# Block products of a seven-product multiply: where their results lie in PSUM, and a planning margin for the side work's TensorE steps

## The chip, the cores and the metric

The kernel runs on one core of one Trainium2 chip. The metric is the device time of one execution in microseconds (us); less is better. Several executions are timed, and their median is the kernel's time. One more execution is recorded by the hardware profiler, and all rows of the profile come from that one.

## The reference

The program is one inference step of a two-layer recurrent decoder trunk for 512 prompt tokens and 8 sample tokens, which the kernel treats as 520 columns. The change lies in layer 1 (HGRN2). Cut to what matters:

```python
def layer_c(h, p, s_c, lb, norm_w, w_in, c_norm_w, w_out, ple_w, ple_g):
    u = rmsnorm(h, norm_w) @ w_in
    q, fx, v, gate = jnp.split(u, [HK_C, 2 * HK_C, 2 * HK_C + D_C], axis=-1)
    g = jnp.logaddexp(jnp.log(lb), jnp.log1p(-lb) + jax.nn.log_sigmoid(fx))
    k = (1.0 - lb) * jax.nn.sigmoid(-fx)
    ...
    o, new_c = hgrn2_scan(q * (DK_C ** -0.5), k, v, g, s_c)
    o = o * lax.rsqrt(jnp.mean(o * o, axis=-1, keepdims=True) + EPS)
    o = o.reshape(Bsz, L, D_C) * c_norm_w * jax.nn.silu(gate)
    h = h + o.astype(h.dtype) @ w_out
    ...
```

There are 16 heads of 128 channels each, so `w_in` is a 1024 x 8192 matrix in four parts q, f, v and g (gate) of 2048 columns. The numbers are 32-bit floats.

## The kernel before

**Layout and precision.** Activations lie with channels on the 128 partitions and the 520 tokens along the free axis. To multiply 32-bit floats, each operand is split into a high and a low part of the type that TensorE takes at its faster rate (`fp32r`), and three products are summed: high x high, high x low, low x high. The split of a weight tile is an ACT cast (`whi` or, from layer 1 on, `whir`) and a DVE subtraction (`wlo`, `wlor`). These go through a small ring of buffers (`ring_space`, line 640; `split_half`, line 645).

**Layer 1** (`layer1_fast`, line 1611) works on pairs of heads, `pr` = 0 to 7. For each pair it makes the projections f, v, q and g; then `decay` computes the decays of the pair, `head` does the chunked recurrence of one head, and `samples` does the 8 sample tokens of the pair. After pairs 2, 4 and 6, inside `pair`, `chunk` multiplies finished heads with the output matrix; the rest follows at the end (`o7`, `o8`).

**The seven-product multiply.** For pairs 1 to 7, f and v are not computed as plain products. `strassen` (line 1705) takes the weights of the two heads, 1024 x 256, as 2 x 2 blocks of 512 x 128, and the activations, 1024 x 520, as 2 x 2 blocks of 512 x 260. Seven block products then do what eight would do in the plain way; the price is additions of blocks before (in DVE, on the weights: `s2`, `s3` and two in place) and after (the results p1 to p7 are copied or added into the pair's tiles `l1a` for f and `l1b` for v). One block product (`product`) is 4 steps over k, each with three matmuls of 128 x 128 by 128 x 260 that add up in PSUM. One call of `strassen` makes f and v of a pair, so 14 block products, n = 0 to 13, in the order p1, p6, p7, p2, p5, p3, p4, first for f, then for v. There are seven calls, 98 block products and 1176 matmuls in all. In the profile their result is the tile `sm`.

**PSUM.** There are two kinds of places. `mmps` gives a tile of two halves of 512 words each (`[128, 2, 512]`), and two such tiles take turns (tag `mm`). All main products use them: a plain product has its 520 columns in the two halves, 260 each. `grab` gives one of four single places of 512 words (`ax0` to `ax3`, called banks in the planner) for the side work: the tiles `A`, `kt`, `kv`, `o`, `ot` and `vt` of the heads, `vs` and `os` of the samples. Before the change, `strassen` opens a new two-half tile for every second product: products 0 and 1 lie in the halves of one tile, 2 and 3 in the next, and so on.

**What sets the order.** The kernel records all operations and a planner (`Plan`, line 210) then lays out the instruction queues. It simulates all engines with a table of costs (`COST`) and takes at each moment the ready operation with the smallest due time `prio`. Main products (`block(True)`) advance a position `pos` by their length; side work is given an offset to that position (`side(start, rate)`), and `urgency` draws it forward where a main product depends on it. Dependencies in the plan go by overlapping regions (`_meet`), so the two halves of a tile are independent there. A new `mm` tile waits for all users of the tile two before it. For a single place, `hold_banks` also asks that all that its readers need from earlier has been queued before its first use; a product that finds no place free is passed over for the moment (`pick`). The resulting order of each engine is fixed in the program; on the chip each engine goes through its queue in order and waits on semaphores that the framework under the kernel sets by its own dependency tracking.

**The margin.** `later(spare)` marks the operations recorded under it. When such an operation runs on TensorE and depends on one of another engine, the planner takes it to be ready `spare` us later than it would be. Nothing is added to the program; only the order changes. Before the change it is used in layer 0 only (0.5, 4.0 and 1.0).

The heads' five TensorE steps, in order, are `A` (scores), `kt` (transposes), `kv`, `o` and `ot` (transposes), and between them lie steps of DVE, ACT and POOL. The TensorE steps of `samples` are `vs`, `os` and a small `ot..s`.

Of the kernel before, what the change touches and what calls it, by code (L numbers as in the profile page):

```python
# [26 lines left out]
HN = N // 2  # L27
# [182 lines left out]
class Plan:  # L210
# [31 lines left out]
    @contextmanager  # L242
    def side(self, start=0.0, rate=0.0, pinned=False):

        keep = self.shift, self.rate, self.pinned
        self.shift, self.rate, self.pinned = start, rate, pinned
        yield
        self.shift, self.rate, self.pinned = keep
# [15 lines left out]
    @contextmanager  # L264
    def block(self, main=False):

        self.open = Op(self, self.pos + self.shift, 0)
        self.open.forms["pe"] = [[], 0.0, None]
        self.open.main = main
        self.open.ins, self.open.outs = [], []  # L270
        yield
        op, self.open = self.open, None
        op.forms["pe"][1] /= 2400.0
        self.add(op, op.ins, op.outs)
# [261 lines left out]
V_LATE, DECAY_LATE, SAMPLE_LATE, HEAD_LATE = 6.67, 0.0, 2.75, -9.44  # L536
HEAD_I, HEAD_RATE, N1_LATE = 6.15, 0.14, -61.78
# [3 lines left out]
def hybrid_decode_step_kernel(ctx: ExitStack, tc: tile.TileContext, I, O, mode="both"):  # L541
# [18 lines left out]
    plans = [Plan(engines, pools, [f"ax{i}" for i in range(4)])]  # L560
    act, dve, pool, pe, sp = (Engine(plans, k) for k in ("act", "dve", "pool", "pe", "sp"))
    side, block = (lambda *a, **k: plans[-1].side(*a, **k)), (lambda *a: plans[-1].block(*a))

    def new(pool_, shape, tag, name, bufs=1, dt=F32):
        return plans[-1].tile(pool_, shape, dt, tag, name, bufs, {"psm": PSUM, "psa": PSUM, "drp": DRAM}.get(pool_, SBUF))
# [4 lines left out]
    def mmps(name):  # L570
        return new("psm", [128, 2, 512], "mm", name, 2)

    def grab(name):

        return new("psa", [128, 512], "ax", name)
# [10 lines left out]
    def tt(out, a, b, op, eng=dve):  # L586
        eng.tensor_tensor(out=out, in0=a, in1=b, op=op)
# [13 lines left out]
    def copy(out, in_):  # L601

        plans[-1].record(("act", "copy", (out, in_), {}), ("dve", "tensor_copy", (out, in_), {}))
# [25 lines left out]
    def load_group(g):  # L629
        ap, k0, kk, c, w = groups[g]  # L630
        r = new("wp", [128, 2048], "raw", f"wraw{g}", 2)
        v = r[:, :kk * w].rearrange("p (k c) -> p k c", k=kk)
        with side(*((plans[-1].shift, 0.0, True) if plans[-1].pinned else (-LOAD_AHEAD,))):
            sp.dma_start(out=v, in_=ap[k0 * 128:(k0 + kk) * 128, c:c + w].rearrange("(k p) c -> p k c", p=128))
        raw_of[g] = v
# [9 lines left out]
    def split_half(v):  # L645

        hv, lv = (r.rearrange("p (k c) -> p k c", k=4) for r in ring_space(1))
        with side(-SPLIT_AHEAD):
            act.copy(hv, v)
            tt(lv, v, hv.bitcast(F32), SUB)  # L650
        return hv, lv
# [300 lines left out]
    mx, e0, e1, sm, lb, omlb, lb60, oml60, lbf, omf, cneg, cq, ch, fb = (lbt[:, i] for i in range(14))  # L952
# [658 lines left out]
    def layer1_fast():  # L1611
# [92 lines left out]

        def strassen(pr, names):

            ps, n = None, 0

            def product(u, x):
                nonlocal ps, n  # L1710
                if n % 2 == 0:
                    ps = mmps(f"sm{pr}_{n // 2}")
                out = ps[:, n % 2, :HN]
                n += 1
                hw, lw = u
                for k in range(4):
                    with block(True):
                        for i, (w, b) in enumerate(((hw, x[0]), (hw, x[1]), (lw, x[0]))):
                            pe.matmul(out, lhsT=w[:, k], rhs=b[:, k], start=(k == 0 and i == 0), stop=(k == 3 and i == 2))
                    plans[-1].pos += 0.334  # L1720
                return out

            def steps(nm):
                e, e1 = 2 * pr, 2 * pr + 1
                start, done = (start_f, done_f) if nm == "f" else (start_v, done_v)
                o0, o1 = start(e), start(e1)
                l0, r0, l1, r1 = o0[:, :HN], o0[:, HN:], o1[:, :HN], o1[:, HN:]
                g = units[sec[f"{nm}{pr}"]][0]
                if g not in raw_of:
                    load_group(g)  # L1730
                v = raw_of[g]
                a11, a12, a21, a22 = v[:, :4, :128], v[:, 4:, :128], v[:, :4, 128:], v[:, 4:, 128:]
                s2, s3 = (new("cst", [128, N], "sgt", f"{nm}{pr}s{i}", 2)[:, :512].rearrange("p (k c) -> p k c", k=4)
                          for i in range(2))
                w = split_half(a11)
                with side(-SPLIT_AHEAD):
                    tt(s3, a11, a21, ADD)
                    tt(a21, a21, a22, ADD)
                    tt(s2, a21, a11, ADD)
                p1 = product(w, x11)  # L1740
                copy(l0, p1)
                p6 = product(split_half(s2), u2)
                tt(r0, l0, p6, ADD)
                p7 = product(split_half(s3), t3)
                tt(l1, p7, r0, SUB)
                w = split_half(a12)
                with side(-SPLIT_AHEAD):
                    tt(a12, a12, s2, ADD)
                p2 = product(w, x21)
                tt(l0, l0, p2, ADD)  # L1750
                p5 = product(split_half(a21), u1)
                tt(r1, l1, p5, SUB)
                tt(r0, r0, p5, ADD)
                p3 = product(split_half(a12), x22)
                tt(r0, r0, p3, ADD)
                done(e)
                p4 = product(split_half(a22), u4)
                tt(l1, l1, p4, ADD)
                done(e1)

            for nm in names:
                steps(nm)
# [147 lines left out]
        def pair(pr, names):  # L1910
            a = 2 * pr
            if pr:
                strassen(pr, names[:2])
                with side(DECAY_LATE):
                    decay(a)
                names = names[2:]
            for nm in names:
                ev = {"f": evac_f, "v": evac_v, "q": evac_q, "g": evac_g}[nm]
                tiles = [(sec[f"{nm}{pr}"] + i, 0, ev(a + i), f"{nm}{a + i}") for i in range(2)]
                if pr == 0 and nm == "f":  # L1920
                    project_both(tiles, XN, K8)
                else:
                    for t in tiles:
                        project_both([t], XN, K8)
                if nm == "f":
                    with side(DECAY_LATE):
                        decay(a)
                if nm == "q" and pr in (2, 4, 6):
                    chunk(f"o{pr}", 2 * pr - 4, 2 if pr == 6 else 4, add_to_h)

        for pr in range(8):
            pair(pr, "fvqg")
            with side(SAMPLE_LATE):
                samples(2 * pr)
            for i in range(2):
                with side(HEAD_LATE + i * HEAD_I, HEAD_RATE):
                    head(2 * pr + i)
        last, o_ = None, last
        chunk("o7", 10, 4, add_to_h)
# [184 lines left out]
    def layer1_end(pl1, ytk, ytk4, keep, pre):  # L2124
# [49 lines left out]
        for half, (sl, blocks) in enumerate(HALVES):  # L2174
# [16 lines left out]
            for i in blocks[:2]:  # L2191
# [5 lines left out]
        act.dma_start(out=O["y_s"].rearrange("b o d -> (b o) d"), in_=ytk4[120:])  # L2197

    layer1_fast()
    layer1_end(slot("xa", "pl1"), slot("w", "ytk", [128, 4160])[:, :4 * D].rearrange("p (i d) -> p i d", i=4),  # L2200
               new("cst", [128, D], "misc", "ytk4"),
# [53 lines left out]
```

## Time and profile before

| | |
|---|---|
| median of 3 runs | 1092.01 us (1089.67 to 1096.3) |
| the profiled execution's own time | 1095.35 us |
| its span, first to last instruction | 1093.6 us |
| TensorE busy (matmul), share of the span | 95% |
| TensorE busy (weight loads) | 92% |
| VectorE (DVE) busy | 78% |
| ScalarE (ACT) busy | 54% |
| GpSimd (POOL) busy | 13% |
| mean granted TensorE clock | 0.992 |
| from and to HBM | 125 GB/s over the span |

PE is the matmul row of TensorE and PEld its weight-load row, which overlaps it. The page also shows the span in 40 equal slices of 27.3 us; each digit is the busy share in tenths:

```profile
PE   8999899999999999999998998989999999999995
PEld 8889898899999999999888998989989889899995
DVE  6788788998977556897797877788867789878863
ACT  6588775645563122555474635455455546564553
```

Layer 0 takes the slices up to about the 17th. Pairs 1 to 7 of layer 1 lie between the 19th and the 38th. PE drops to 8 in several slices of layer 1. The groups of the block products, by what they read, among the costliest groups of the page (busy us, mean ns of one, then idle time of the engine just before them and what ended most of it):

```profile
L520 PE MATMUL sm<-uh,whir 128*128 128x260 f32 x224 | 65.6, 293 | 8.3 <-DVE l1b L520 5.7
L520 PE MATMUL sm<-xh,whir 128*128 128x260 f32 x168 | 50.9, 303 | 14.0 <-DVE l1a L520 14.0
L520 PE MATMUL sm<-ul,whir 128*128 128x260 f32 x224 | 63.4, 283 | 0.0
L520 PE MATMUL sm<-uh,wlor 128*128 128x260 f32 x224 | 63.2, 282 | 0.0
```

All operations are recorded by one helper, so every row has its line (L520), and groups are told apart by their tiles. `xh`, `xl` and `uh`, `ul` are high and low parts of the activation blocks and of their combinations; `whir` and `wlor` are high and low parts of the weights. The first of the three matmuls of a k-step reads `uh` or `xh` with `whir`; the idle time stands before these alone.

### The profile page before, as it was taken

To read this page: it belongs to the slowest core of one execution; us is meant where nothing else is said; L and a number is where in the kernel's file an instruction comes from. 1 tells how busy PE (TensorE), PEld (TensorE's weight loads), DVE (VectorE), ACT (ScalarE), POOL (GpSimd) and SP (SyncE) were. 2 spreads that over 40 slices of the span, in tenths; PEclk is the share of its full clock that TensorE was granted. 3 is DMA by queue.
4 is the path that set the end of the run, shared out by engine and by line. 5 is a ranking of instruction groups with operands and counts; after the bars stand their busy time and mean duration, and the time that the engine had idled before them with its cause. 6 is when DMAs were issued, how large, how long until landed. Compare 5 with 4: busy or idle time off the path is not lost.

```text
span 1093.6 us, 21305 instructions
## 1 busy us (share of the span) xinstructions
PE 1037.6 (95%) x8427; PEld 1005.2 (92%) x8427; DVE 852.5 (78%) x1727; ACT 593.4 (54%) x1310; POOL 142.8 (13%) x241
## 2 busy tenths in 40 slices
PE   8999899999999999999998998989999999999995
PEld 8889898899999999999888998989989889899995
DVE  6788788998977556897797877788867789878863
ACT  6588775645563122555474635455455546564553
POOL 4635845100000000010000000001010010100000
PEclk9999899999999999999999999999999999999998
DMA  8612263346693333723424351434432443354311
GB/s 276 235 39 78 79 180 115 117 134 177 211 278 130 116 107 120 239 82 86 144 67 119 119 157 42 119 85 133 123 107 89 104 130 103 103 182 140 103 53 43
DMA packets 129956, 138.44 MB, mean 127 GB/s; under 512 B 13704, under 2 KB 111128, under 8 KB 129832
## 3 DMA queue, kind: packets, MB, share of 16 engines
q1 hardware_dynamic: 129464, 136.64, 40.8%
q8 instruction: 68, 1.11, 0.4%
q10 hardware_dynamic: 160, 0.30, 0.1%
q14 instruction: 40, 0.33, 0.1%
q0 software_dynamic: 224, 0.06, 0.0%
HBM read 111.71 MB, written 25.44 MB: 125 GB/s over the span
## 4 chain that ended last, share of the span: by engine, by line
PE 74%; DVE 9%; DMA 6%; POOL 4%; ACT 4%; issue 2%; SPq 0%; POOLq 0%; ACTq 0%; DVEq 0%
PE sm L520 14%; PE o L520 10%; PE g L520 9%; PE pg L520 8%; PE q L520 6%; PE ob L520 4%; PE z L520 3%; DVE l1a L520 3%; PE xbc L520 2%; PE ag L520 2%; PE ax L520 2%; PE pl L520 2%; POOL csm L520 1%; DVE wlo L520 1%; PE A L520 1%
## 5 line engine op out<-in xcount | busy, mean ns | idle before, releaser
L520 ACT CAST whir<-wraw 128x512 fp32r<-128x512 f32 (+1 forms) x121 | 96.5, 800 | 112.2 <-PE sm L520 43.8
L520 DVE TENSOR_TENSOR wlor<-wraw,whir 128x512 fp32r<-128x512 f32 (+1 forms) x121 | 109.7, 911 | 13.5 <-ACT whir L520 12.2
L520 POOL TENSOR_TENSOR at__1738<-at__1738,nhalf 128x4 f32<-128x4 f32 (+1 forms) x24 | 24.9, 1037 | 496.8 <-DVE at__1738 L520 496.8
L520 PE MATMUL o<-ohl,whir 128*128 128x260 f32 x512 | 84.6, 288 | 1.6 <-DVE l1a L520 1.2
L520 ACT CAST whi<-wraw 128x1024 fp32r<-128x1024 f32 (+1 forms) x56 | 57.7, 1031 | 49.9 <-PE ob L520 34.6
L520 DVE TENSOR_TENSOR wlo<-wraw,whi 128x1024 fp32r<-128x1024 f32 (+1 forms) x64 | 77.3, 1208 | 9.3 <-ACT whi L520 8.8
L520 PEld LDWEIGHTS o<-ohl,whir 128*128 128x128 f32 x512 | 71.2, 191 | 2.9 <-ACT whir L520 1.4
L520 PE MATMUL sm<-uh,whir 128*128 128x260 f32 x224 | 65.6, 293 | 8.3 <-DVE l1b L520 5.7
L520 PE MATMUL sm<-xh,whir 128*128 128x260 f32 x168 | 50.9, 303 | 14.0 <-DVE l1a L520 14.0
L520 PE MATMUL sm<-ul,whir 128*128 128x260 f32 x224 | 63.4, 283 | 0.0
L520 PE MATMUL sm<-uh,wlor 128*128 128x260 f32 x224 | 63.2, 282 | 0.0
L520 PE MATMUL g<-xh,whir 128*128 128x260 f32 x256 | 54.2, 293 | 0.6 <-DVE l1a L520 0.6
L520 PE MATMUL q<-xh,whir 128*128 128x260 f32 x256 | 53.8, 291 | 0.0
L520 PEld LDWEIGHTS sm<-uh,whir 128*128 128x128 f32 x224 | 42.1, 188 | 12.2 <-DVE l1b L520 8.0
L520 PE MATMUL o<-ohl,wlor 128*128 128x260 f32 x256 | 51.9, 284 | 0.0
L520 PE MATMUL q<-xh,wlor 128*128 128x260 f32 x256 | 51.5, 283 | 0.0
L520 PE MATMUL q<-xl,whir 128*128 128x260 f32 x256 | 51.5, 283 | 0.0
L520 PE MATMUL g<-xh,wlor 128*128 128x260 f32 x256 | 51.4, 282 | 0.0
L520 PE MATMUL g<-xl,whir 128*128 128x260 f32 x256 | 51.4, 282 | 0.0
L520 PEld LDWEIGHTS sm<-xh,whir 128*128 128x128 f32 x168 | 31.6, 188 | 20.2 <-DVE l1a L520 19.6
L520 PE MATMUL sm<-xl,whir 128*128 128x260 f32 x168 | 47.5, 283 | 0.0
L520 PE MATMUL sm<-xh,wlor 128*128 128x260 f32 x168 | 47.4, 282 | 0.0
(592 smaller groups left out, 3472.9 us busy)
## 6 DMA issues: line engine op xcount, KB each, us to landing
wraw<-in_c_w_in_dram SPq DMA_DIRECT2D x32, 1024.0 KB
wraw<-in_ab_w_in_dram SPq DMA_DIRECT2D x15, 1024.0 KB
wraw<-in_ab_w_out_dram SPq DMA_DIRECT2D x8, 1024.0 KB
wraw<-in_ple_gate_dram SPq DMA_DIRECT2D x8, 1024.0 KB
wraw<-in_c_w_out_dram SPq DMA_DIRECT2D x8, 1024.0 KB
pl<-pl_d SPq DMA_DIRECT2D x2, 2080.0 KB
smp<-in_state_b_ssm_dram SPq DMA_DIRECT2D x8, 512.0 KB
acy<-acsT_d SPq DMA_DIRECT2D x8, 512.0 KB
```

What stands on the lines that cost most here:

```text
L520: getattr(f, name)(*a, **k)
```

## The change

In `strassen`, the place of a block product is chosen by its number modulo 6. Products 0 and 3 of six lie in the two halves of one `mm` tile, 1 and 4 in the halves of the next, and 2 and 5 in single places of the side work, under the name `sg` and the product's number. Each call of `strassen` so opens six `mm` tiles where it opened seven (at n = 0, 1, 6, 7, 12 and 13; the last two are used by half), and takes four single places (n = 2, 5, 8 and 11). What is computed, and the order in which the products are recorded, stay as they were.

In the loop over the pairs, the operations of `samples` and `head` are recorded under `later(0.6)`.

```diff
         def strassen(pr, names):
 
-            ps, n = None, 0
+            pss, n = [], 0
 
             def product(u, x):
-                nonlocal ps, n
-                if n % 2 == 0:
-                    ps = mmps(f"sm{pr}_{n // 2}")
-                out = ps[:, n % 2, :HN]
+                nonlocal n
+
+                i = n % 6
+                if i % 3 == 2:
+                    out = grab(f"sg{pr}_{n}")[:, :HN]
+                else:
+                    if i < 2:
+                        pss[i:] = [mmps(f"sm{pr}_{n}")]
+                    out = pss[i % 3][:, i // 3, :HN]
                 n += 1
                 hw, lw = u
                 for k in range(4):
...
         for pr in range(8):
             pair(pr, "fvqg")
-            with side(SAMPLE_LATE):
+            with side(SAMPLE_LATE), plans[-1].later(0.6):
                 samples(2 * pr)
             for i in range(2):
-                with side(HEAD_LATE + i * HEAD_I, HEAD_RATE):
+                with side(HEAD_LATE + i * HEAD_I, HEAD_RATE), plans[-1].later(0.6):
                     head(2 * pr + i)
```

## The prediction

> **What bounds the kernel now.** I read the page first, then the waits of TensorE in the layer that the change touches, then the timeline around one such wait, and last the busy times of all engines in the seven stretches of block products. The page:
>
> ```profile
> span 1093.6 us, 21305 instructions
> PE 1037.6 (95%) x8427; PEld 1005.2 (92%) x8427; DVE 852.5 (78%) x1727; ACT 593.4 (54%) x1310; POOL 142.8 (13%) x241
> PE 74%; DVE 9%; DMA 6%; POOL 4%; ACT 4%; issue 2%; SPq 0%; POOLq 0%; ACTq 0%; DVEq 0%
> ```
>
> TensorE (PE) is busy for 95% of the span and carries 74% of the chain that ended last. Time is won by taking away gaps on PE, and won in full only as long as no other engine takes PE's place. The gaps between 511 and 1050 us, where pairs 1 to 7 of layer 1 run (who waited for whom: us in total, times, longest):
>
> ```profile
> PE sm L520 <- DVE l1a L520: 14.0, 27, 0.5
> PE sm L520 <- DVE l1b L520: 5.7, 11, 0.5
> PE ot L520 <- DVE l1a L520: 2.4, 3, 1.3
> PE sm L520 <- ACT l1a L520: 2.3, 5, 0.5
> PE o L520 <- DVE l1a L520: 1.2, 1, 1.2
> PE vs L520 <- DVE at__1738 L520: 1.0, 1, 1.0
> PE g L520 <- DVE l1a L520: 0.6, 1, 0.6
> ```
>
> The block products (tile sm) wait 27 + 11 + 5 = 43 times for 14.0 + 5.7 + 2.3 = 22.0 us. All other waits here come to 5.2 us. One of the 43, from the timeline (start, us, engine; at the end the idle time before):
>
> ```profile
> 516.80 0.28 PE L520 MATMUL sm<-uh,wlor 128*128 128x260 f32 x1
> 516.92 0.29 PE L520 MATMUL sm<-xh,whir 128*128 128x260 f32 x1
> 517.04 0.29 PE L520 MATMUL sm<-xl,whir 128*128 128x260 f32 x1
> 517.16 0.28 PE L520 MATMUL sm<-xh,wlor 128*128 128x260 f32 x1
> 517.48 0.43 DVE L520 TENSOR_TENSOR l1a<-sm,l1a 128x260 f32<-128x260 f32 x1 [0.50 <-PE sm L520]
> 517.97 0.39 PE L520 MATMUL sm<-xh,whir 128*128 128x260 f32 x1 [0.52 <-DVE l1a L520]
> 518.19 0.29 PE L520 MATMUL sm<-xl,whir 128*128 128x260 f32 x1
> ```
>
> At 516.80 the last matmul of product p7 starts; it ends at 517.08. From 516.92 PE already writes the first three matmuls of p2, into the other half of the same tile. DVE reads p7's result only at 517.48, 0.04 us after p2's third matmul ends (517.16 + 0.28 = 517.44) and 0.40 after its own product ended. PE goes on with p2 at 517.97, when DVE has read. Yet p2's fourth matmul has the weights of a unit already in use, and another half of PSUM. So reader and writer are ordered by the tile, not by the half. That is the step on which the forecast stands.
>
> What one wait costs is read from starts, since matmuls overlap: 517.04 to 517.16 is the pitch, 0.12 us; from 517.16 to 518.19, two matmuls on, it takes 1.03 where 0.24 would do, thus 0.79 us. For 43 waits that is 34.0 us, more than the 22.0 us of the waits table. Cross-check by the seven stretches from the first to the last block product of a call, first row and sum (columns: us, busy us and instructions of PE, PEld, DVE, ACT, POOL, then PE clock, DMA share, GB/s):
>
> ```profile
> 511.78:537.62 25.84, 22.27 (x171) 20.81 (x171) 19.44 (x43) 10.08 (x22) 1.03 (x1) 1.00 0.40 119
> ...
> 931.47:959.95 28.48, 26.27 (x211) 24.86 (x210) 23.34 (x49) 17.51 (x42) 3.14 (x3) 1.00 0.41 111
> sum 187.37, PE 165.09 PEld 154.46 DVE 143.57 ACT 92.59 POOL 7.20; mean PE 23.58 PEld 22.07 DVE 20.51 ACT 13.23 POOL 1.03
> ```
>
> They last 187.4 us. Seven calls x 14 products x 12 matmuls at 0.12 us are 141.1 us. The side work on PE in them is little (171 - 168 = 3 matmuls in the first, 43 in the last). About 35 to 40 us are left, which the 34.0 us of waits mostly explain. The clock there is 1.00, so nothing is to be won from it.
>
> **The change part by part.**
>
> *Products n and n+1 no longer share a tile.* By n % 6, products 0 and 3 share one tile, 1 and 4 the other, 2 and 5 get single banks of the side work. Between two products of one tile lie two others, 2 x 12 x 0.12 = 2.9 us, against a read of 0.43 us that can start 0.04 us after its product. All 43 waits should go: **-34.0 us**. The number of matmuls, reads and splits is unchanged; no DMA is issued or moved by the diff. But the planner lays out all queues afresh from about the first head on, SP's and POOL's too. There is cover for that: the loads of the next weights are released by the splits, which come earlier along with PE. The two waits on them (DVE, 511 to 1050 us) follow the splits that release the loads and move with them, so I cost them at nothing; if they doubled, it would be 4.7 us:
>
> ```profile
> DVE f2s L520 <- DMA wraw<-in_c_w_in_dram: 2.7, 1, 2.7
> DVE f3s L520 <- DMA wraw<-in_c_w_in_dram: 2.0, 1, 2.0
> ```
>
> *What is late next: DVE.* In the seven stretches DVE has 143.57 us of work. With 34.0 us gone they last 153.4 us, and DVE is busy for 93.6% of it, where it was 76.6%. The trace has one stretch where DVE is as full beside a busy PE, in layer 0, and a longer one that is less full:
>
> ```profile
> 191.40:246.00 54.60, 53.03 (x449) 47.91 (x450) 53.01 (x105) 31.59 (x88) 5.16 (x4) 1.00 0.40 126
> 145.00:340.00 195.00, 189.89 (x1579) 181.10 (x1578) 172.93 (x325) 116.95 (x336) 26.50 (x39) 1.00 0.57 177
> PE sbt L520 <- DVE acy L520: 1.6, 1, 1.6
> PE st L520 <- DVE acy L520: 0.3, 1, 0.3
> ```
>
> In 191 to 246 us DVE runs at 97%, and PE waits for it for 1.9 us of 54.6 (the last two rows). The same share of 153.4 us is 5.3 us. Bounds: 0, if the order keeps the splits ahead; and, if DVE reached only the 88.7% of the second row, 143.57 / 0.887 = 161.9, so 8.5 us. I take **+5.3 us**, since 97% is the nearest share. Queued behind a late DVE are the reads of the next products and the splits of the next weights, and behind these PE itself, in order.
>
> *Every third product in a bank of the side work.* There are four such banks. Four products of a call use one (n = 2, 5, 8, 11), 28 in all, each for about 12 x 0.12 + 0.43 = 1.9 us. Side work keeps banks long in these stretches (call 1):
>
> ```profile
> 504.83 1.05 PE L520 MATMUL A<-l1a 128*128 128x128 f32 x8
> 534.09 0.75 DVE L520 COPY_PREDICATED l1d<-l1d,A 128x512 f32<-128x512 uint32 x1
> 511.46 0.28 PE L520 MATMUL os<-l1d 128*16 128x128 f32 x1
> 538.83 0.27 ACT L520 ACTIVATE l1d<-os 16x128 f32<-16x128 f32 x1 [0.19 <-PE os L520]
> 538.60 0.68 DVE L520 TENSOR_TENSOR l1a<-o,at__1738 128x512 f32<-128x512 f32 x1
> ```
>
> A head's A is written at 504.8 and read at 534.1; os is begun at 511.5 and read at 538.8; and o, written before the stretch, is read at 538.6. Three of four banks are taken through most of the call. The fourth suffices, since the products that want it come three apart (4.3 us) and hold it for 1.9. Lower bound 0; upper bound a wait of the kind now seen (0.5) at each of 28, thus 14 us. I take the longest such wait at the four products of call 1 alone, **+2.0 us**, nearer to the lower end because that call is the one where I found three banks taken. No gain can come from this part by itself.
>
> *After the last product.* Products 12 and 13 open two tiles, so the first q product waits for the read of product 12 with one product between (1.44 us) where there were two. The read takes 0.43 us: **0**, and 7 x 0.5 = 3.5 us if DVE is that late.
>
> *The margin of 0.6 us.* In the plan, PE steps of samples and heads become ready 0.6 us later after a step of another engine. Nothing is added on the chip; steps move back in PE's order. It can save up to 0.6 us in each of the waits before ot (three: 1.3, the other two 1.1 together) and vs (1.0): 0.6 + 1.1 + 0.6 = 2.3 us. It can cost: a head has five such steps (A, kt, kv, o, ot), so its chain ends up to 3.0 us later, and where the chain is already last (pairs 1 and 2, where the waits of 1.2 and 1.3 lie) q's evacuation and then g wait for it, 2 x 3.0 = 6.0 us. Cover elsewhere is PE's own products, which run meanwhile. Between -2.3 and +6.0 I take **0**: the small waits point to a gain, the chains to a loss, and no row decides.
>
> Sum: -34.0 + 5.3 + 2.0 = -26.7 us. The profiled execution took 1095.35 us (span 1093.6 and 1.75 around it), so 1068.7; it lies 3.3 above the median of the three runs, 1092.01. On that scale: **1065.3 us**, say 1065.
>
> **The rivals.**
>
> *The waits stay in another form.* "Perfetto Trace Analysis" of the Trainium skill, section Identifying Performance Opportunities, says that the same gap repeating on the engine that should be saturated can mean that there is too little PSUM for the next tile. By that rule the cause would be shortage, and the change adds no PSUM. As a mechanism here: products would wait for a free place, each as now, and the time stays at 1092. The trace speaks against it: PE waits from 517.44 on, after it has already written three matmuls into p2's place (516.92 to 517.16), so the place was free. Chance 0.07.
>
> *DVE takes PE's place.* The plan packs side work of heads and samples into these stretches; if 88.7% is DVE's limit, the banks cost half their bound (7 us), and the first q products 3.5: -34.0 + 8.5 + 7 + 3.5 = -15, thus 1077. For it: 93.6% is asked. Against: at 97% PE lost only 1.9 us in 54.6. Chance 0.13.
>
> *The margin spends the gain.* If the heads' chains ended last in all eight pairs, 8 x 3.0 = 24 us would go to waits of g and of the output chunks: -26.7 + 24 = -2.7, thus 1089. Waits of ot and g show in few pairs. Chance 0.04.
>
> *Slower: a product stuck behind a side bank.* PE runs in order. If the free bank were not there, a product would wait until a low-ranking DVE read (A's came 30 us late) frees one. At 28 products the gain is gone at 34.0 / 28 = 1.2 us each; at a product's own length, 1.44 us, it is 40 us with DVE's 5.3 on top: -34.0 + 40.3 + 5.3 = +11.6, thus 1104. Against: calls 3 and 5 carry little side work, and DVE reads sooner once PE stands. Chance 0.05.
>
> **How the numbers follow.** The forecast (gain of 20 to 39 us) has 0.71. Its best end is all 34.0 us and the 5.2 of the other waits, 39.2, thus 1053. The upper end takes in most of DVE's rival: 12 us of gain, 1080. So 1053 to 1080 holds about 0.8. One per cent, about what a measurement of this kernel can tell from no change, is 10.9 us: faster by more is the forecast and DVE's rival, 0.84; within it are the waits in another form and the margin's rival, 0.11; slower 0.05.
>
> **What would show each step.** Right: no more waits of PE sm on l1a or l1b after three matmuls of a product; the reads of a product start some 0.04 us after its last matmul; the seven stretches last about 155 to 163 us in sum, with DVE above 88%; what waits are left name wlor or whir, or the new tile sg. Wrong in the first step: the same 0.5 us waits before sm, elsewhere in the product. Wrong in the bank's term: PE sg waits for A, os or o readers. Wrong in the margin's: waits before g and the output chunks grow past 5 us. Before 490 us the two traces should agree within a microsecond or two; if they differ there, the plan moved more than I assume.

## The result

| kernel | median us | range | ratio to before, 95% interval |
|---|---|---|---|
| before | 1092.08 | 1089.67 to 1096.3 (4 runs) | |
| changed | 1061.16 | 1057.61 to 1062.69 (4 runs) | 0.9708 [0.9669, 0.9747] |

The change makes the kernel faster by 30.9 us in the medians. The forecast was 1065 (1053 to 1080). The profiled execution of the changed kernel took 1060.69 us, 34.7 less than that of before; that one lay 3.3 above the median of before. Among the experiments further down, one execution of `new_margin_09` took 2556.68 us, and that kernel's median is that of its other three. The page of the changed kernel, with the same lines as before:

```profile
span 1059.0 us, 21367 instructions
PE 1027.7 (97%) x8427; PEld 1004.1 (95%) x8427; DVE 848.9 (80%) x1731; ACT 586.4 (55%) x1304; POOL 140.8 (13%) x241
PE 80%; DVE 6%; POOL 4%; ACT 4%; DMA 3%; issue 2%; SPq 0%; POOLq 0%; ACTq 0%; DVEq 0%
```

PE has as many matmuls as before (8427) and its busy share is 97%. In the chain that ended last, PE's share has gone from 74% to 80%, DVE's from 9% to 6% and DMA's from 6% to 3%. Next, who waited for whom on PE in layer 1, 505 to 1020 us, all rows of the view (us in total, times, longest):

```profile
PE o L520 <- DVE l1a L520: 1.6, 1, 1.6
PE vs L520 <- DVE dtt L520: 1.1, 1, 1.1
PE o L520 <- DVE h L520: 0.8, 1, 0.8
PE kv L520 <- ACT l1b L520: 0.7, 1, 0.7
PE sm L520 <- DVE l1a L520: 0.5, 1, 0.5
PE pg L520 <- DVE wlo L520: 0.3, 1, 0.3
PE sm L520 <- DVE wlor L520: 0.3, 1, 0.3
PE sg L520 <- ACT whir L520: 0.2, 1, 0.2
```

The block products (sm and sg) wait three times for 1.0 us, where they waited 43 times for 22.0. The other waits come to 4.5 us, where they were 5.8 (the 5.2 of the prediction leaves out two rows of 0.3). The same place of the first call as shown before, in the timeline:

```profile
514.92 0.29 PE L520 MATMUL sg<-uh,wlor 128*128 128x260 f32 x1
515.04 0.28 PE L520 MATMUL sm<-xh,whir 128*128 128x260 f32 x1
515.16 0.29 PE L520 MATMUL sm<-xl,whir 128*128 128x260 f32 x1
515.24 0.43 DVE L520 TENSOR_TENSOR l1a<-sg,l1a 128x260 f32<-128x260 f32 x1
515.29 0.28 PE L520 MATMUL sm<-xh,wlor 128*128 128x260 f32 x1
```

At 514.92 the last matmul of p7 starts, ending at 515.21. DVE reads p7, which now lies in a single place (sg), from 515.24, 0.03 us later, while PE writes p2 in another tile. (The planner has moved the first three matmuls of p2 ahead of p7; those from 515.04 on are the following ones.) PE keeps its pitch of 0.12 us all along. Last, the seven stretches from the first to the last block product of a call, in sum:

```profile
sum 160.61, PE 159.51 PEld 154.56 DVE 151.09 ACT 89.71 POOL 9.29; mean PE 22.79 PEld 22.08 DVE 21.58 ACT 12.82 POOL 1.33
```

They took 187.37 us before, so 26.8 less. Adding up the times from one matmul's start to the next gives: waits -27.5 (28.9 before, 1.4 after), the slower first step after each wait -4.3 (4.5 before, 0.3 after), other starts within the products +2.2 (each late by less than the view of waits shows), side work on PE +2.7 (there are 22 more of its matmuls inside the stretches). DVE is now busy for 151.09 / 160.61 = 94.1% of them. The rest of the 34.6 us by which the span fell: 1.6 us lie ahead of layer 1, where nothing was changed (its first matmul starts at 458.1 before and 456.5 after), and the remaining 6.2 lie outside the stretches too, mostly between the calls (5.2), out of which side work moved.

### The profile page after: what moved, and what is told of

Its sections match the earlier page's. It is cut to its first block, busy times and chain, and to the rows that moved or that the text cites. A ratio compares the mean times of both kernels' runs of the same rounds, so it can differ in the third digit from the quotient of the medians.

```text
span 1059.0 us, 21367 instructions
## 1 busy us (share of the span) xinstructions
PE 1027.7 (97%) x8427; PEld 1004.1 (95%) x8427; DVE 848.9 (80%) x1731; ACT 586.4 (55%) x1304; POOL 140.8 (13%) x241
## 4 chain that ended last, share of the span: by engine, by line
PE 80%; DVE 6%; POOL 4%; ACT 4%; DMA 3%; issue 2%; SPq 0%; POOLq 0%; ACTq 0%; DVEq 0%
PE o L520 11%; PE g L520 10%; PE sm L520 9%; PE pg L520 9%; PE q L520 8%; PE ob L520 4%; PE ag L520 4%; PE sg L520 4%; PE z L520 4%; PE xbc L520 2%; PE ax L520 2%; PE pl L520 2%; PE kv L520 1%; PE A L520 1%; POOL csm L520 1%
## 5 line engine op out<-in xcount | busy, mean ns | idle before, releaser
L520 ACT CAST whi<-wraw 128x1024 fp32r<-128x1024 f32 (+1 forms) x56 | 57.7, 1031 | 50.4 <-PE ob L520 34.6
L520 POOL TENSOR_TENSOR at__1738<-at__1738,nhalf 128x4 f32<-128x4 f32 (+1 forms) x24 | 22.5, 941 | 465.2 <-DVE at__1738 L520 465.2
L520 PE MATMUL sm<-uh,whir 128*128 128x260 f32 x140 | 40.8, 291 | 0.5 <-DVE l1a L520 0.5
L520 PEld LDWEIGHTS g<-xh,whir 128*128 128x128 f32 x256 | 39.2, 189 | 0.9 <-issue 0.8
L520 PE MATMUL sm<-xh,whir 128*128 128x260 f32 x140 | 39.9, 285 | 0.0
L520 PEld LDWEIGHTS o<-ohl,wlor 128*128 128x128 f32 x256 | 39.9, 190 | 0.0
L520 PE MATMUL sm<-xh,wlor 128*128 128x260 f32 x140 | 39.6, 283 | 0.3 <-DVE wlor L520 0.3
L520 PEld LDWEIGHTS q<-xh,whir 128*128 128x128 f32 x256 | 39.3, 189 | 0.5 <-issue 0.5
L520 PE MATMUL sm<-uh,wlor 128*128 128x260 f32 x140 | 39.7, 283 | 0.0
L520 PE MATMUL xbc<-xnh,whi 128*128 128x260 f32 x192 | 39.7, 288 | 0.0
```

Of the source, the lines that this page charges most:

```text
L520: getattr(f, name)(*a, **k)
```

## The experiments

Each kernel below differs from the changed one by what its diff shows, if not said otherwise. All are compared with the kernel before on the same chip.

| kernel | median us | ratio to before, 95% interval |
|---|---|---|
| `place_only` | 1061.95 | 0.9721 [0.9706, 0.9735] |
| `margin_only` | 1103.44 | 1.009 [1.007, 1.011] |
| `solo` | 1066.58 | 0.9746 [0.9722, 0.9771] |
| `one_between` | 1065.23 | 0.975 [0.9734, 0.9767] |
| `all_banks` | 1096.56 | 1.0029 [0.9998, 1.0059] |
| `dve_half` | 1074.26 | 0.9833 [0.9796, 0.987] |
| `dve_more` | 1083.08 | 0.9922 [0.989, 0.9954] |
| `new_margin_03` | 1060.41 | 0.9698 [0.9673, 0.9723] |
| `new_margin_09` | 1072.62 | 0.9823 [0.9797, 0.9848] |
| `new_margin_12` | 1081.8 | 0.9894 [0.9851, 0.9936] |
| `one_between_0` | 1070.11 | 0.979 [0.976, 0.982] |
| `solo_0` | 1068.75 | 0.9794 [0.9766, 0.9823] |

### Which half of the change does the work

`place_only` takes the margin away again:

```diff
-            with side(SAMPLE_LATE), plans[-1].later(0.6):
+            with side(SAMPLE_LATE):
                 samples(2 * pr)
...
-                with side(HEAD_LATE + i * HEAD_I, HEAD_RATE), plans[-1].later(0.6):
+                with side(HEAD_LATE + i * HEAD_I, HEAD_RATE):
```

> The new places of the products, no margin for samples and heads. Theory T (the 43 waits come from two products sharing a tile, and the places alone end them): sm and sg wait for less than 2 us in all, time 1060 to 1068. Rival M (the margin does the work, by moving side steps out of the way): the waits before sm stay near 22 us and the time near 1090. The margin's own term was taken as 0 within -2.3 to +6.0 us, so T gives a difference to the changed kernel of that size, with the sign open.

`margin_only` is the kernel before with only the two lines of the margin.

> The old places of the products, with the margin of 0.6 us for samples and heads. Theory T: some 43 waits of 0.5 us before sm as before, time 1086 to 1096. Rival M: the waits go, time near 1062.

The places alone give the whole gain: 1061.95 against 1061.16 with the margin, intervals that overlap. Its products wait twice, for 0.7 us in all. Rival M falls. The margin alone makes the kernel slower, by 0.9%, where 1086 to 1096 us was expected. Its waits, 480 to 1070 us, the first rows and the last one of sm:

```profile
PE sm L520 <- DVE l1a L520: 14.0, 27, 0.5
PE sm L520 <- DVE l1b L520: 9.2, 13, 3.0
PE sm L520 <- ACT l1a L520: 3.2, 7, 0.5
PE g L520 <- DVE l1a L520: 2.5, 1, 2.5
PE g L520 <- DVE h L520: 1.6, 1, 1.6
PE sm L520 <- DVE at__1738 L520: 0.5, 1, 0.5
```

The old waits of sm are all there, 48 now for 26.9 us, and waits before g have come to 4.1 us where there was one of 0.6.

### Why the waits were there

`solo` and `one_between` use fewer places than the changed kernel, and no single bank:

```diff
-                i = n % 6
-                if i % 3 == 2:
-                    out = grab(f"sg{pr}_{n}")[:, :HN]
-                else:
-                    if i < 2:
-                        pss[i:] = [mmps(f"sm{pr}_{n}")]
-                    out = pss[i % 3][:, i // 3, :HN]
+                out = mmps(f"sm{pr}_{n}")[:, 0, :HN]
```

> Each product in the first half of a tile of its own; the second half stays unused, and no single bank is taken. So the products have two places in turn where they had four before and eight after. Theory T: no two products share a tile, and a tile's next use comes two products later (one product of 1.44 us between, against a read of 0.43): waits before sm under 3 us, time 1060 to 1068. Rival S (the waits were a shortage of PSUM): with half the places the waits grow, time above 1092.

```diff
-                i = n % 6
-                if i % 3 == 2:
-                    out = grab(f"sg{pr}_{n}")[:, :HN]
-                else:
-                    if i < 2:
-                        pss[i:] = [mmps(f"sm{pr}_{n}")]
-                    out = pss[i % 3][:, i // 3, :HN]
+                i = n % 4
+                if i < 2:
+                    pss[i:] = [mmps(f"sm{pr}_{n}")]
+                out = pss[i % 2][:, i // 2, :HN]
```

> Products 0 and 2 share a tile, 1 and 3 the next, so one product lies between neighbours, and no single bank is taken. The same four places as before, in another order. Theory T: the read (0.43 us, 0.04 after its product) fits into the 1.44 us of the product between; waits under 3 us, time 1060 to 1068. If the distance of two products and the third bank are needed, waits of some tenths remain at many products: 5 us or more, time 1066 to 1080. Rival S: the same places, so the same waits, near 1092.

`solo` gives the products half the places they had before, and the waits are gone: the block products wait twice, and these are all its rows of sm:

```profile
PE sm L520 <- ACT l1b L520: 0.2, 1, 0.2
PE sm L520 <- DVE l1b L520: 0.2, 1, 0.2
```

Shortage of PSUM (rival S) is ruled out: less of it, well used, is enough. `one_between` has exactly the places of before in another order, and its sm waits are three for 0.9 us:

```profile
PE sm L520 <- ACT l1a L520: 0.5, 1, 0.5
PE sm L520 <- DVE l1b L520: 0.4, 2, 0.2
```

Both bear out theory T, and a distance of one product suffices for the waits. Both are some 4 to 5 us slower than the changed kernel in the medians, though the intervals of the ratios overlap with its own. Their traces show waits elsewhere: the largest row of each is a wait before a head's last transposes, 4.9 us in `solo` and 4.2 in `one_between`, where the changed kernel has none. In the timeline of `solo`:

```profile
551.62 1.09 PE L520 MATMUL ot<-ident,l1a 128*128 128x128 f32 x4 [4.93 <-DVE l1a L520]
```

and, in the timeline of `one_between`:

```profile
546.63 0.63 PE L520 MATMUL ot<-ident,l1a 128*128 128x128 f32 x4 [4.20 <-DVE l1a L520]
```

So the distance of two and the third place are not needed against the waits. Whether the few us by which the plan that comes with them looks better are due to the places themselves, or to the accident of a plan, these runs don't tell.

### What a bank of the side work costs

```diff
+                out = grab(f"sg{pr}_{n}")[:, :HN]
```

`all_banks` puts this line in the place of the choice by n % 6.

> All 98 products in the four single places that the heads and samples use; the two-half tiles stay with the plain products. Theory T (a product waits for the reader of its own tile only): neighbours never share a tile, so the 43 waits are gone; what is left is competition for places. If the bank's term of the prediction was rightly small, side work gives way: time 1058 to 1070, waits before sg under 5 us. Rival (a product gets stuck behind a place whose low-ranking reader is late, as A's was by 30 us): one wait of 1 us or more at every second product, 98 / 2 x 1 = 49 us, time above 1090.

At 98 products in place of 28 the time is the rival's: 1096.56, no faster than before. But its size came about in another way than it was put. These are all the waits of products, 480 to 1060 us:

```profile
PE sg L520 <- DVE l1a L520: 10.7, 6, 3.2
PE sg L520 <- ACT l1d L520: 3.7, 3, 1.2
PE sg L520 <- DVE at__1738 L520: 2.6, 2, 1.3
PE sg L520 <- DVE wlor L520: 1.9, 3, 1.5
```

They are 14 waits for 18.9 us, where the rival had put 49 waits of 1 us. `all_banks` is 35 us slower than the changed kernel; the rest lies in other waits of PE (10.3 us, where they were 4.5) and, by an estimate in the last section, some 12 us in the clock. The longest wait of a product, in the timeline of PE:

```profile
575.60 0.28 PE L520 MATMUL sg<-uh,wlor 128*128 128x260 f32 x1
579.05 0.39 PE L520 MATMUL sg<-xh,whir 128*128 128x260 f32 x1 [3.17 <-DVE l1a L520]
```

and what DVE did at the end of that time, in the timeline of DVE:

```profile
578.05 0.34 DVE L520 SCALAR_TENSOR_TENSOR l1d<-l1c,l1d 128x128 f32<-128x128 f32 x1
578.32 0.68 DVE L520 TENSOR_TENSOR l1a<-o,at__1738 128x512 f32<-128x512 f32 x1
```

PE stands from 575.9 until DVE has read a head's o at 579.0, to which it comes only after a string of steps of the samples. That is the mechanism that the prediction's slower rival named: a product behind a place whose reader ranks low. Three of the 14 waits, of 3.17, 3.17 and 2.57 us, end with the read of an o. In the changed kernel no product waits for a side reader; the one wait of sg is for a weight cast.

### How near DVE is to its limit

```diff
                 copy(l0, p1)
+                tt(l0, l0, l0, MAX)
...
                 tt(l1, p7, r0, SUB)
+                tt(l1, l1, l1, MAX)
...
                 tt(r1, l1, p5, SUB)
+                tt(r1, r1, r1, MAX)
```

This is `dve_half`; `dve_more` has such a line after the first use of each of the seven products.

> The changed kernel with one more DVE pass (maximum of a block with itself, 128x260, some 0.34 us) after three of the seven results, 42 in all, 14.3 us of DVE work in the seven stretches. They have 160.6 us with DVE busy for 151.1. Theory D (DVE is the next bound of the stretches): 165.4 us of DVE work no longer fit, time up by 5 us at 100% DVE and 10 us at 97%, 1066 to 1071. Rival E (the plan moves side work of DVE out of the stretches, and PE stays the bound): up by less than 3 us, near 1061 to 1064.

> The same after all seven results, 98 passes, 33.3 us of DVE work. Theory D: 151.1 + 33.3 = 184.4 us of DVE work in 160.6 us, so up by 24 us at 100% and 29 us at 97%, 1085 to 1091, with waits of sm and sg on wlor. Rival E: up by less than 10 us, since DVE is idle for 20% of the whole span.

`dve_half` is up by 13.1 us, about the 14.3 us of DVE work that was added. The seven stretches of `dve_half` in sum (windows; columns as before):

```profile
sum 176.49, PE 164.20 PEld 155.17 DVE 165.73 ACT 91.52 POOL 11.68; mean PE 23.46 PEld 22.17 DVE 23.68 ACT 13.07 POOL 1.67
```

and those of `dve_more`:

```profile
sum 183.08, PE 162.61 PEld 153.87 DVE 169.84 ACT 89.08 POOL 12.90; mean PE 23.23 PEld 21.98 DVE 24.26 ACT 12.73 POOL 1.84
```

165.73 / 176.49 is 93.9%, as in the changed kernel (94.1%), while PE's share fell from 99% to 93%. So with this work added DVE holds the stretches, where in the changed kernel PE, busy for 99%, still held them: at 94% DVE has next to no slack left, and the 14.3 us pass through nearly one for one. `dve_more` is up by 21.9 us for 33.3 us added. DVE's work in its stretches grew by 169.84 - 151.09 = 18.8 us, so 14.5 us of work left them. Theory D is borne out in direction, but neither time lies in its range: 1074.26 is above 1066 to 1071, and 1083.08 below 1085 to 1091. The 14.5 us that left the stretches bear out rival E in part for the larger dose. Nor are the longest waits in `dve_more` those on wlor that were expected (3.1 us); they are waits of sm on l1b, 9.7 us. One rival was not tested: the passes stand between the reads of the products and lengthen that chain too. That DVE's share stays at 93 to 94% with more work speaks for its total, but does not exclude the chain.

### The margin

`new_margin_03`, `_09` and `_12` are the changed kernel with 0.3, 0.9 and 1.2 in place of 0.6:

> The changed kernel with twice the margin, 1.2 us. Without the margin it was 1061.95, with 0.6 us 1061.16. Theory N (with the new places the margin only reshuffles side work; its effect is small and has no direction): 1058 to 1068. Rival C (each margin delays the heads' chains, five steps each): twice 0.6 us more at each step, waits before g and the output chunks grow, time 1068 to 1085.

> The changed kernel with a margin of 0.3 us. So far: 0 gave 1061.95, 0.6 gave 1061.16, 1.2 gave 1081.8. Theory C (a margin delays the heads' chains, and this costs once their slack is used up): 0.3 lies before that point, 1058 to 1065. Rival R (every margin gives another plan, and plans scatter by some 10 us without an order): anywhere between 1055 and 1085.

> The changed kernel with a margin of 0.9 us. Theory C: between the two ends, 1061 to 1082, with waits before g and the output chunks above the 2.4 us of the margin 0.6. Rival R: anywhere between 1055 and 1085, under 1061 too.

With the new places 0, 0.3 and 0.6 us cannot be told apart (1061.95, 1060.41, 1061.16); 0.9 gives 1072.62 and 1.2 gives 1081.8. So there is a point beyond which the margin costs, as theory C has it. The first rows of `new_margin_12` show where: before g and the output chunks, and before steps of the side work itself.

```profile
PE g L520 <- DVE h L520: 6.0, 1, 6.0
PE os L520 <- DVE l1d L520: 3.9, 2, 3.4
PE o L520 <- DVE h L520: 2.6, 4, 1.2
PE A L520 <- DVE l1a L520: 2.6, 2, 1.4
```

`one_between_0` and `solo_0` are the two placements above without the margin.

> One product between neighbours of a tile, no single bank, no margin. With the margin it was 1065.23, with one wait of 4.2 us before a head's last transposes (ot) and two before an output chunk (2.0). Theory C: without the margin the heads' chains are shorter, so these shrink, 1058 to 1065. Rival R: between 1055 and 1085 in either direction. If it comes out under 1058, the single banks are not worth having.

> Each product in the first half of a tile of its own, no margin. With the margin it was 1066.58, with one wait of 4.9 us before ot. Theory C: 1058 to 1066. Rival R: between 1055 and 1085 in either direction.

Here theory C fails: without the margin both are no faster (1070.11 against 1065.23, 1068.75 against 1066.58; the intervals of both pairs overlap barely). Both then have a wait before g on the output chunk's addition, 4.0 and 4.8 us, in exchange for the one before ot. So at 0.6 us the effect has no fixed sign: +11 us with the old places, nothing with the new ones, and about -5 and -2 with the two others. Rival R, that plans scatter by some 10 us, is not excluded. With the old places the waits of PE grow by 6.8 us in all, with 4.9 more before sm and 3.5 more before g, while others get shorter; why they grow so much there stays open. A plan that does not know of the 43 waits may be hurt more by steps placed late, but no run tested that.

## Why the prediction was right

**The waits go, -34.0 us.** Right in mechanism and in size. 43 waits became three; by the starts they were worth 33.4 us with the slower steps after them, and 1.7 are left. `place_only`, `solo` and `one_between` show that sharing a tile by neighbours was the cause, and reading 0.79 us per wait from starts, not 0.52 from the waits view, was needed to get the size: by the waits view the most to be won from them was 22 us, less than the 26.8 won in the stretches.

**DVE late next, +5.3 us.** The direction was right, the size was not: at 94.1% of DVE, where 93.6% was forecast, products waited for 1.0 us in all by the view of waits, and lost at most 3.9 by the starts (1.7, and the 2.2 of other starts). The estimate was taken over from a stretch of layer 0 at 97%, whose two waits were of another kind of step. What the term meant, that DVE would be the next to bind, is borne out by `dve_half`.

**A bank for every third product, +2.0 us.** Mis-sized: 0. No product waited for a side reader. That the price exists, and where it decides, shows in `all_banks`.

**After the last product, 0.** Right: q has no wait in the changed kernel.

**The weights' loads, 0.** Right for PE. The waits on them moved to other places and are somewhat longer, 5.6 us in DVE where there were 4.7, and 2.3 in ACT where there were none; the rows of the changed kernel, 505 to 1020 us:

```profile
DVE v5s L520 <- DMA wraw<-in_c_w_in_dram: 2.4, 1, 2.4
ACT whir L520 <- DMA wraw<-in_c_w_in_dram: 2.3, 1, 2.3
DVE f2s L520 <- DMA wraw<-in_c_w_in_dram: 1.4, 1, 1.4
DVE f5s L520 <- DMA wraw<-in_c_w_in_dram: 1.2, 1, 1.2
DVE f4s L520 <- DMA wraw<-in_c_w_in_dram: 0.6, 1, 0.6
```

**The margin, 0.** Right at 0.6 us with these places, but by luck: no row decided for 0. Its bounds, -2.3 to +6.0, were not bounds for the edit as such: with the old places it cost 11 us.

**The sum.** -26.7 was forecast; -30.9 was measured in the medians and -34.7 in the profiled executions. The terms were worked out for the stretches, and there the sum came out as forecast, -26.8, but in part by luck. The waits were worth 33.4 for 34.0, DVE and the banks together cost at most 3.9 for 7.3, and the side work that moved into the stretches cost 2.7, which the prediction had put at nothing; these errors nearly cancel. What the forecast is short of lies outside the stretches, where it counted nothing: 1.6 us ahead of layer 1 and 6.2 elsewhere, out of which those 2.7 us had moved.

**The rivals.** That the waits stay in another form is ruled out by `solo`: with half the places the products wait for 0.4 us. The Trainium skill ("Perfetto Trace Analysis", section Identifying Performance Opportunities) says that the same gap repeating can mean too little PSUM. That is not what it meant here. DVE did not take PE's place (PE is busy for 99% of the stretches), and the margin did not spend the gain (no wait before g is left). A product behind a side bank appears only in `all_banks`.

## What to carry to other kernels

When TensorE waits for the reader of another result after it has already begun to write its own, see whether the two share something that the program tracks as one. Here it was a tile of two halves, and giving neighbours different tiles ended the wait, even with less PSUM. The price of such a wait is to be read from the starts of the matmuls on either side of it. With PE's gaps closed, the next to hold the stretch was here the engine whose busy time had come nearest to the new length, DVE; work added to it showed how little slack was left.

## What the runs showed of the hardware

TensorE ran at half clock for 3.41 us at a time after some gaps of a few us. In `all_banks` a gap of 3.17 us is followed by a stretch at clock 0.50 (windows; PE clock is the third column from the end):

```profile
575.60:579.00 3.40, 0.28 (x3) 0.07 (x1) 3.40 (x13) 0.62 (x1) 0.00 (x0) 1.00 0.22 46
580.20:583.60 3.40, 3.40 (x16) 2.67 (x15) 2.02 (x6) 1.24 (x4) 0.54 (x1) 0.50 0.78 223
```

The products' matmuls in it start 0.22 us apart, where they start 0.12 apart at full clock. In the changed kernel two waits of 1.12 and 1.65 us next to each other (601 to 604 us) are followed by 0.55. In `all_banks` the clock over the seven stretches is 0.90 to 0.95, where it is 1.00 in the changed kernel: it has nine such half-clock times in layer 1, the changed kernel one. By the two pitches the eight more cost 8 x 3.41 x (1 - 0.12 / 0.22), some 12 us. That is an estimate. The waits of 4.93 and 4.20 us in `solo` and `one_between` are followed by 0.50 as well. But not every such gap is: in `dve_more` a wait of 2.23 us ends at 670.07, and the clock stays at 1.00:

```profile
670.10:673.50 3.40, 3.40 (x28) 3.40 (x29) 3.40 (x8) 3.20 (x5) 0.00 (x0) 1.00 0.71 206
```

So a gap of a few us can cost more than its own length; these runs show no length from which it always does.
